# Gate stores on ACT's queue, loads in program order where the branch products begin, sums of h in program order, the first tile's norm weight by channel

## The chip, the cores and the metric

One core of one Trainium2 chip. The metric is the device time of one execution in microseconds (us). A core has TensorE (PE, matmuls), VectorE (DVE), ScalarE (ACT), GpSimd (POOL), SyncE (SP, which here only issues DMAs) and 16 DMA engines.

## What is computed

One layer of a decoder with three parallel mixers, 1024 tokens by 1024 channels, all in float32. Cut to what matters:

```python
h = RMSNorm_pre(x)                       # x * rsqrt(mean(x^2)) * g_pre
q,k,v,z_a, u,v_s,z_s, z_m,xBC,dt, gates = split(h @ W_in)
y_att = sliding_window_attention(q, k, v) * silu(z_a)
y_sg  = spatial_gate(u, v_s) * silu(z_s)
y_ssm = RMSNorm(ssd(conv(xBC), dt) * silu(z_m))
merged = sum_i sigmoid(gate_i) * (y_i @ W_br_i)
out = x + RMSNorm_post(merged @ W_out)
```

## The kernel before

Every float32 matrix is split into a high part (ACT casts it) and a low part (DVE subtracts, POOL for some of the weights), and a product is three matmuls per 128-channel step: high by high, high by low, low by high. TensorE executes its instructions in the order in which the program writes them. For the other engines the tile framework picks an order of its own, except inside `tc.manual_schedule(engines=...)`, where the engines named keep the program's order too.

The stages, in the order of TensorE:

1. Opening. Eight tiles of 128 tokens: `load_x` (L384), `norm` (sum of squares on ACT L392, `rs` on DVE and POOL, `hh` = x times `rs` times `gpre` on DVE L399), `flip` (eight transposes by TensorE L407, high part by ACT L410, low part by DVE L411). The first products (L141 to L143, weights `w_first`) begin as soon as tile 0 stands in `h`. The norm weight `gpre` is copied to all partitions by two DMAs that SP issues right behind the first tile of x.
2. Attention, with products of q, z_a, v_s and the gates filled in between; the last of the fillers are two `gate_unit`s (L116 to L118), whose results ACT takes out of PSUM into `vst` (L353).
3. Sums of h (L790 to L816). The products that follow use a scheme with seven products for eight (`PairStream`, L225 on), and need sums of blocks of h: for each of four steps `kt`, DVE makes four `r` (L797: high plus low part), POOL makes `x1` to `x4` from them (L800 to L803), and three of these are split into the blocks `S` (`split`, ACT L688 and DVE L689), the fourth later into the block `hB[1,0]`. `r` has one buffer each, `x1`, `x2`, `x4` two. Behind the four steps the first four weights of the stream are prepared (`whi` by ACT L253, `wlo` by DVE L228, differences of weights by POOL L223). The first pair product is L289 to L291.
4. The SSD chunks with pair products in between; DVE, ACT, POOL and SP keep the program's order here. Some of the pair products are gate logits: `tanh` on ACT (L693), and a store of 256 KB to `gate_dr` from SP's queue (L695), 44 of them. `evac` stores other results (L707).
5. The spatial gate (L1005 to L1060), whose results `yts` are stored to `y_dr` (L1043).
6. Branch products. `load_y` brings `y_dr` blocks back (SP L1080) and splits them (ACT L1091, DVE L1092), for y0 and y1 ahead of the loop and y2 to y7 behind the pools' change. The first unit of `br_unit` takes y0 and y1, then y2 and y3, and so on (L116 to L118). `load_w` (L93 to L100) brings its weights; `raw`, `whi` and `wlo` have three buffers each, which it shares with `PairStream`.
7. The product with `w_out`, the last norm and the store.

Of the kernel before, what the change touches and what calls it, by code (L numbers as in the profile page):

```python
# [11 lines left out]
F32 = mybir.dt.float32  # L12
# [28 lines left out]
def hybrid_kernel(ctx, tc, t, out):  # L41
# [24 lines left out]
    one = mhalf_row[:, 1:2]  # L66
    dsk, ng, bcv = mhalf_row[:, 2:18], mhalf_row[:, 18:34], mhalf_row[:, 34:58]
    bst = const.tile([P, NB, 4, 8], F32, name="bst")
    ssum = const.tile([P, 32], F32, name="ssum")
    acs, etot, dth, edec = (const.tile([P, NB, 32], F32, name=nm) for nm in ("acs", "etot", "dth", "edec"))  # L70

# [11 lines left out]
    def bcast_load(dst, src):  # L83
        nc.sync.dma_start(out=dst, in_=src.unsqueeze(0).broadcast_to([P, src.shape[-1]]))
# [287 lines left out]
    if True:  # L372

        with tc.tile_pool(name="xp", bufs=1) as xp:
# [5 lines left out]
            def load_x(tt):  # L380
                xt = xp.tile([P, D], F32, name="xt", bufs=2)
                for i in range(1 if tt else 2):
                    f = slice(i * 512, (i + 1) * 512) if tt == 0 else slice(0, D)
                    nc.sync.dma_start(out=xt[:, f], in_=t["x"][tt * P:(tt + 1) * P, f])  # L384
                return xt

            def norm(tt, xt):
                sq = xp.tile([P, D], mybir.dt.bfloat16, name="sq", bufs=1)
                ss = xp.tile([P, 2], F32, name="ss", bufs=2)
                for i in range(2):  # L390
                    f = slice(i * 512, (i + 1) * 512)
                    A.activation(sq[:, f], xt[:, f], AF.Square, accum_out=ss[:, i:i + 1])  # L392
                rs = xp.tile([P, 1], F32, name="rs", bufs=2)
                V.tensor_tensor(rs, ss[:, 0:1], ss[:, 1:2], op=ALU.add)
                rsqrt(rs, rs, 1.0 / D)
                hh = xp.tile([P, D], F32, name="hh", bufs=3)
                for i in range(2):
                    f = slice(i * 512, (i + 1) * 512)
                    V.scalar_tensor_tensor(hh[:, f], xt[:, f], rs, gpre[:, f], op0=ALU.mult, op1=ALU.mult)  # L399
                return hh  # L400

            def flip(tt, hh):
                for i in range(2):
                    ps = psum(ps_tr, "tr")
                    for j in range(4):
                        k = i * 4 + j
                        T.transpose(ps[:, j * P:(j + 1) * P], hh[:, k * P:(k + 1) * P], ident)  # L407
                    src = ps.rearrange("p (k s) -> p k s", k=4)
                    dst = [h[:, :, tt % 4 * P:(tt % 4 + 1) * P] for h in hB[tt // 4, i]]
                    A.copy(dst[0], src)  # L410
                    V.tensor_tensor(dst[1], src, dst[0].bitcast(F32), op=ALU.subtract)  # L411

            xts = {0: load_x(0)}
            for i in range(2):
                bcast_load(gpre[:, i * 512:(i + 1) * 512], t["g_pre"][i * 512:(i + 1) * 512])
            wfirst, hh = [], {}

            def first_w(i):
# [2 lines left out]
            with tc.manual_schedule(engines={mybir.EngineType.DVE, mybir.EngineType.Activation}):  # L421
                hh[0] = norm(0, xts.pop(0))
                first_w(0)
                first_w(1)
                xts[1] = load_x(1)
                flip(0, hh.pop(0))
                first_w(2)
                hh[1] = norm(1, xts.pop(1))
                first_w(3)
# [261 lines left out]
    def gate_pair(n):  # L691
        def tanh(b, d):
            A.activation(d, d, AF.Tanh, scale=0.5)  # L693
            i, half = NGATE + 2 * n + b % 10 - 1, b // 10 - 1
            nc.sync.dma_start(out=gate_dr[i, :, half * 512:(half + 1) * 512], in_=d)  # L695
            yield from ()

        def evac(b, d, after):
            pst.fresh.append(tanh(b, d[:, 4:]))
        return [t["w_gp"][n][k] for k in range(2)], evac  # L700
# [86 lines left out]
            pst.add(conv_pair(g, next(cv)) if kind == "x" else z_pair(g, next(z)) if kind == "z"  # L787
                    else zu_pair(next(zu)) if kind == "u" else gate_pair(next(gates)))

    with tc.tile_pool(name="bp", bufs=1, reuse_waits="tile") as bp:  # L790
        made = []
        for kt in range(5):
            if kt < 4:
                r = {}
                for ij, h in hB.items():
                    r[ij] = bp.tile([P, 512], F32, name="r%d%d" % ij)
                    V.tensor_tensor(r[ij], h[0][:, kt, :].bitcast(F32), h[1][:, kt, :].bitcast(F32), op=ALU.add)  # L797
                x1, x2, x4 = (bp.tile([P, 512], F32, name=f"x{i}", bufs=2) for i in (1, 2, 4))
                x3 = bp.tile([P, 512], F32, name="x3", bufs=4)
                G.tensor_tensor(x1, r[1, 0], r[1, 1], op=ALU.add)  # L800
                G.tensor_tensor(x2, x1, r[0, 0], op=ALU.subtract)
                G.tensor_tensor(x3, r[0, 0], r[1, 0], op=ALU.subtract)
                G.tensor_tensor(x4, r[0, 1], x2, op=ALU.subtract)  # L803
                made.append((x1, x2, x3, x4))
            st.fill(10.4)
            if kt > 0:
                x1, x2, _, x4 = made[kt - 1]
                for to, x in ((s1, x1), (s2, x2), (s4, x4)):
                    split(to, kt - 1, x)
        st.drain()  # L810

        for q in range(pst.AHEAD):
            pst._prepare(q)
        pst.prepared = pst.AHEAD
        for kt in range(4):
            split(hB[1, 0], kt, made[kt][2])  # L816
# [257 lines left out]
    def raw_tile(m):  # L1074
        return (py if m % 4 < 2 else pz).tile([P, S], F32, name=f"yraw{m % 4 // 2}", bufs=2)
# [42 lines left out]
        return ct_unit(t["w_br"][un * 8 + dd], rhs, evac, (2, 4, 5, 6, 7, KT) if k == dd == 0 else (KT,))  # L1118

    br = [br_unit(k, dd) for k in range(4) for dd in range(8)]  # L1120
    for n in range(NPY):
        ys[n] = load_y(n)
    st.add(*br[:8])
    st.loaded = st._load()
    pst.run(4)
    while pst.fresh or pst.waiting or pst.active:
        pst._work()
    es7.close()
    ph1.close()
    pz = ctx.enter_context(tc.tile_pool(name="pz", bufs=1, reuse_waits="tile"))  # L1130
    pools.append(pz)

    for n in (9, 10, 11):
        spare[n] = slot(n)
    pz.tile([P, 384], F32, name="pz_pad")
    for n in (5, 6, 7, 8):
        spare[n] = slot(n)
    merged.extend(pz.tile([P, S], F32, name=f"mg{i}") for i in range(4))
    for n in (2, 3):
        raws[n] = raw_tile(n)  # L1140
    for n in (2, 3, 4):
        spare[n] = slot(n)
    merged.extend(pz.tile([P, S], F32, name=f"mg{i}") for i in range(4, 8))
    for n in range(NPY, 8):
        ys[n] = load_y(n)
    for un in range(4):
        st.fill(5.2 * 8)
        if un < 3:
# [52 lines left out]
def _layout(inp):  # L1201
# [36 lines left out]
    for nm in ("q", "za"):  # L1238
# [2 lines left out]
    o["w_br"] = np.concatenate([ct(wb[:1024], 8), ct(wb[1024:], 8), ct(a["w_br_att"][0], 8),  # L1241
                                ct(a["w_br_sg"][0], 8)], 0)
    o["g_pre"] = a["norm_pre"][0]
    o["g_post"] = a["norm_post"][0]
    o["rel"] = a["rel_bias"][_buckets()].transpose(0, 2, 1)
    o["sinks"] = a["att_sinks"][0]
# [28 lines left out]
```

## Time and profile before

| | us |
|---|---|
| runs of the kernel before | 6930.69, 1812.04, 1818.29 |
| median of these | 1818.29 |
| profiled execution, its own time | 1813.3 |
| span of that execution | 1811.6 |
| TensorE busy in the span | 1744.7 |
| mean granted clock of TensorE | 0.99 |

The span is what the trace covers, from the first to the last instruction; the profiled execution's own time is 1.7 us longer. In the trace every instruction has a start, a length, its line and, in square brackets, how long its engine was idle before it and who ended that idle time. The rows that are used stand in a section below.

### The profile page before, as it was taken

To read this page: it belongs to the slowest core of one execution; us is meant where nothing else is said; L and a number is where in the kernel's file an instruction comes from. 1 tells how busy PE (TensorE), PEld (TensorE's weight loads), DVE (VectorE), ACT (ScalarE), POOL (GpSimd) and SP (SyncE) were. 2 spreads that over 40 slices of the span, in tenths; PEclk is the share of its full clock that TensorE was granted. 3 is DMA by queue.
4 is the path that set the end of the run, shared out by engine and by line. 5 is a ranking of instruction groups with operands and counts; after the bars stand their busy time and mean duration, and the time that the engine had idled before them with its cause. 6 is when DMAs were issued, how large, how long until landed. Compare 5 with 4: busy or idle time off the path is not lost. (4 is left out here: it accounts for less than half of the span.)

```text
span 1811.6 us, 26027 instructions
## 1 busy us (share of the span) xinstructions
PE 1744.7 (96%) x9181; PEld 1470.6 (81%) x9181; DVE 1271.1 (70%) x1781; ACT 842.0 (46%) x1883; POOL 843.7 (47%) x761
## 2 busy tenths in 40 slices
PE   7999999998999999999999999999889999999997
PEld 6888888897888877877887788887767888888897
DVE  6456676658998988899788978886775374444424
ACT  5245555534556666766577665542232212111221
POOL 1015566656665786777678765656324050000000
PEclk9999999999999999999999999999999999999999
DMA  6121111122334556445654564544786353533204
GB/s 228 63 79 48 47 59 40 52 82 67 105 105 145 164 176 197 144 129 171 196 160 141 162 194 153 166 137 125 245 277 242 108 189 125 171 116 93 82 24 163
DMA packets 165378, 243.28 MB, mean 134 GB/s; under 512 B 13153, under 2 KB 105601, under 8 KB 165121
## 3 DMA queue, kind: packets, MB, share of 16 engines
q1 hardware_dynamic: 165248, 241.63, 41.9%
q8 instruction: 73, 1.20, 0.3%
q14 instruction: 57, 0.46, 0.1%
HBM read 177.99 MB, written 63.59 MB: 133 GB/s over the span
## 5 line engine op out<-in xcount | busy, mean ns | idle before, releaser
L228 DVE TENSOR_TENSOR wlo<-raw,whi 128x512 fp32r<-128x512 f32 x195 | 193.6, 994 | 24.8 <-ACT whi L253 21.3
L116 PE MATMUL ps_mm<-y,whi 128*128 128x512 f32 x512 | 201.0, 393 | 7.7 <-ACT y L1091 7.7
L117 PE MATMUL ps_mm<-y,whi 128*128 128x512 f32 x512 | 201.1, 393 | 2.0 <-DVE y L1092 2.0
L118 PE MATMUL ps_mm<-y,wlo 128*128 128x512 f32 x512 | 200.6, 392 | 0.0
L289 PE MATMUL ps_mm<-h,whi 128*128 128x512 f32 x468 | 192.4, 411 | 3.7 <-ACT vst L353 3.7
L98 ACT CAST whi<-raw 128x1024 fp32r<-128x1024 f32 (+1 forms) x69 | 71.5, 1038 | 248.6 <-PE ps_mm L117 233.2
L291 PE MATMUL ps_mm<-h,wlo 128*128 128x512 f32 x468 | 183.0, 391 | 0.0
L290 PE MATMUL ps_mm<-h,whi 128*128 128x512 f32 x468 | 182.8, 391 | 0.0
L253 ACT CAST whi<-raw 128x512 fp32r<-128x512 f32 x195 | 118.8, 613 | 93.2 <-POOL raw L223 72.3
L89 POOL TENSOR_TENSOR rso<-rso,mhalf_row 128x1 f32<-128x1 f32 x8 | 4.4, 545 | 323.2 <-DVE rso L88 323.2
L289 PE MATMUL ps_mm<-S,whi 128*128 128x512 f32 x352 | 142.1, 404 | 4.6 <-DVE tp L301 3.5
L753 DVE SCALAR_TENSOR_TENSOR acc<-tp,wcv,acc 128x512 f32<-128x512 f32 x144 | 145.1, 1027 | 1.7
L291 PE MATMUL ps_mm<-S,wlo 128*128 128x512 f32 x352 | 137.5, 391 | 1.8 <-DVE wlo L228 1.8
L290 PE MATMUL ps_mm<-S,whi 128*128 128x512 f32 x352 | 137.3, 390 | 0.0
L223 POOL TENSOR_TENSOR ts<-raw 128x512 f32<-128x512 f32 x78 | 123.9, 1589 | 17.0 <-DVE wlo L228 12.4
L116 PE MATMUL ps_mm<-h,whi 128*128 128x512 f32 x304 | 120.9, 398 | 1.2 <-ACT vst L353 1.2
L116 PEld LDWEIGHTS ps_mm<-y,whi 128*128 128x128 f32 x512 | 96.9, 189 | 28.8 <-ACT y L1091 8.8
L1115 DVE SCALAR_TENSOR_TENSOR tm<-gld,ps_mm 128x512 f32<-128x512 f32 x48 | 32.9, 686 | 123.1 <-PE ps_mm L118 123.1
L117 PE MATMUL ps_mm<-h,whi 128*128 128x512 f32 x304 | 118.6, 390 | 0.0
L118 PE MATMUL ps_mm<-h,wlo 128*128 128x512 f32 x304 | 118.5, 390 | 0.0
L117 PEld LDWEIGHTS ps_mm<-y,whi 128*128 128x128 f32 x512 | 96.9, 189 | 23.6 <-DVE y L1092 3.6
L118 PEld LDWEIGHTS ps_mm<-y,wlo 128*128 128x128 f32 x512 | 97.1, 190 | 20.2
(242 smaller groups left out, 4873.5 us busy)
## 6 DMA issues: line engine op xcount, KB each, us to landing
seg<-acs_dr SPq DMA_DIRECT2D x64, 256.0 KB, 4.2
raw<-in_w_br_dram SPq DMA_DIRECT2D x32, 512.0 KB, 4.4
yraw<-y_dr SPq DMA_DIRECT2D x32, 512.0 KB, 4.7
gld<-gate_dr SPq DMA_DIRECT2D x32, 512.0 KB, 3.5
raw<-in_w_xbc_dram SPq DMA_DIRECT2D x24, 512.0 KB, 3.9
raw<-in_w_gp_dram SPq DMA_DIRECT2D x22, 512.0 KB, 4.4
gate_dr<-tp SPq DMA_DIRECT2D x44, 256.0 KB, 3.4
raw<-in_w_zm_dram SPq DMA_DIRECT2D x16, 512.0 KB, 4.5
```

Source lines behind the costliest of these rows:

```text
L98: A.copy(hi, raw)
L116: T.matmul(ps, lhsT=whi[:, ks], rhs=rhs(0, kt, half), start=kt == 0, stop=False)
L117: T.matmul(ps, lhsT=whi[:, ks], rhs=rhs(1, kt, half), start=False, stop=False)
L118: T.matmul(ps, lhsT=wlo[:, ks], rhs=rhs(0, kt, half), start=False, stop=kt == KT - 1)
L223: G.tensor_tensor(b[out], b[x], b[y], op=ALU.subtract)
L228: V.tensor_tensor(lo, src, hi.bitcast(F32), op=ALU.subtract)
L253: A.copy(hi, src)
L289: T.matmul(o, lhsT=hi[:, ks], rhs=h0, start=kt == 0, stop=False)
L290: T.matmul(o, lhsT=hi[:, ks], rhs=h1, start=False, stop=False)
L291: T.matmul(o, lhsT=lo[:, ks], rhs=h0, start=False, stop=kt == 3)
L753: V.scalar_tensor_tensor(acc, d[:, 1 + tap:513 + tap], wcv[:, ti, tap:tap + 1], acc, op0=ALU.mult, op1=ALU.add)
L1115: V.scalar_tensor_tensor(tm, gt[0][:, fs], 1.0, ps, op0=ALU.add, op1=ALU.mult)
```

## The change

Four edits:

- The 44 stores of gates (256 KB each) are issued from ACT's queue, behind the `tanh` that writes the data, and not from SP's.
- From the first `load_y` to the last before the branch loop, SP keeps the program's order.
- In the section with the sums of h, DVE, ACT and POOL keep the program's order.
- Tile 0 leaves the norm weight out of `hh`. `flip` applies it behind the transpose, where a channel is a partition: eight ACT instructions with a per-partition scale and eight DVE instructions, each 128x128, in place of two and two of 128x512. The weight comes as `gcol`, eight columns of 128 numbers placed into a free column of `bst`, by one DMA of 1024 separate 4-byte elements behind x0. `gpre` is loaded by one DMA behind tile 1 of x.

```diff
+    gcol = bst[:, :, 0, 6:7]
...
-                    V.scalar_tensor_tensor(hh[:, f], xt[:, f], rs, gpre[:, f], op0=ALU.mult, op1=ALU.mult)
+                    if tt == 0:
+                        V.tensor_scalar(hh[:, f], xt[:, f], rs, None, op0=ALU.mult)
+                    else:
+                        V.scalar_tensor_tensor(hh[:, f], xt[:, f], rs, gpre[:, f], op0=ALU.mult, op1=ALU.mult)
...
-                    A.copy(dst[0], src)
-                    V.tensor_tensor(dst[1], src, dst[0].bitcast(F32), op=ALU.subtract)
+                    if tt == 0:
+                        for j in range(4):
+                            g = gcol[:, i * 4 + j, :]
+                            A.activation(dst[0][:, j, :], src[:, j, :], AF.Copy, scale=g)
+                            V.scalar_tensor_tensor(dst[1][:, j, :], src[:, j, :], g, dst[0][:, j, :].bitcast(F32),
+                                                   op0=ALU.mult, op1=ALU.subtract)
+                    else:
+                        A.copy(dst[0], src)
+                        V.tensor_tensor(dst[1], src, dst[0].bitcast(F32), op=ALU.subtract)
...
             xts = {0: load_x(0)}
-            for i in range(2):
-                bcast_load(gpre[:, i * 512:(i + 1) * 512], t["g_pre"][i * 512:(i + 1) * 512])
+            nc.sync.dma_start(out=gcol, in_=t["g_col"])
...
                 xts[1] = load_x(1)
+                bcast_load(gpre, t["g_pre"])
...
-            nc.sync.dma_start(out=gate_dr[i, :, half * 512:(half + 1) * 512], in_=d)
+            nc.scalar.dma_start(out=gate_dr[i, :, half * 512:(half + 1) * 512], in_=d)
...
-    with tc.tile_pool(name="bp", bufs=1, reuse_waits="tile") as bp:
+    with tc.tile_pool(name="bp", bufs=1, reuse_waits="tile") as bp, tc.manual_schedule(
+            engines={mybir.EngineType.DVE, mybir.EngineType.Activation, mybir.EngineType.Pool}):
...
-    for n in range(NPY):
-        ys[n] = load_y(n)
-    st.add(*br[:8])
-    st.loaded = st._load()
-    pst.run(4)
+    with tc.manual_schedule(engines={mybir.EngineType.SP}):
+        for n in range(NPY):
+            ys[n] = load_y(n)
+        st.add(*br[:8])
+        st.loaded = st._load()
+        pst.run(4)
...
-    for n in range(NPY, 8):
-        ys[n] = load_y(n)
+        for n in range(NPY, 8):
+            ys[n] = load_y(n)
```

TensorE's order is the same in both kernels. The other engines' orders differ at three places.

ACT in the section with the sums of h, before. `S` from `x` is the high part of a sum, `vst` what comes out of the gate units, `whi` from `raw` or `ts` (L253) a weight of the stream:

```order
L253 CAST whi<-raw 128x512
L362 COPY vst<-ps_mm 128x256
L253 CAST whi<-raw 128x512
L688 CAST S_4292<-x_4561 128x512
L688 CAST S_4290<-x_4562 128x512
L688 CAST S_4294<-x_4563 128x512
L353 ACTIVATE vst<-ps_mm 128x256 x2
L688 CAST S_4292<-x_4645 128x512
L688 CAST S_4290<-x_4646 128x512
L688 CAST S_4294<-x_4647 128x512
L253 CAST whi<-ts 128x512
L353 ACTIVATE vst<-ps_mm 128x256 x2
```

The same place after, from the second gate unit's `vst` on (L354, L700 and L254 are L353, L688 and L253 of before):

```order
L354 ACTIVATE vst<-ps_mm 128x256 x4
L700 CAST S_4304<-x_4456 128x512
L700 CAST S_4302<-x_4457 128x512
L700 CAST S_4306<-x_4458 128x512
L700 CAST S_4304<-x_4575 128x512
L700 CAST S_4302<-x_4576 128x512
L700 CAST S_4306<-x_4577 128x512
L700 CAST S_4304<-x_4659 128x512
L700 CAST S_4302<-x_4660 128x512
L700 CAST S_4306<-x_4661 128x512
L254 CAST whi<-raw 128x512 x3
```

All four `vst` of the second gate unit now stand ahead of the `S` of the second, third and fourth step, and the stream's first weight stands behind the last of them; before, two weights were cast ahead of the third step's `S`.

DVE at the same section, after (before, the twelve `r` of the second to fourth step stand where their buffers allow, between the `S`):

```order
L701 TENSOR_TENSOR S_4305<-x_4456,S_4304 128x512
L701 TENSOR_TENSOR S_4303<-x_4457,S_4302 128x512
L701 TENSOR_TENSOR S_4307<-x_4458,S_4306 128x512
L810 TENSOR_TENSOR r_4651<-h_105,h_106 128x512
L810 TENSOR_TENSOR r_4653<-h_107,h_108 128x512
L810 TENSOR_TENSOR r_4655<-h_109,h_110 128x512
L810 TENSOR_TENSOR r_4657<-h_111,h_112 128x512
```

and before:

```order
L797 TENSOR_TENSOR r_4559<-h_111,h_112 128x512
L689 TENSOR_TENSOR S_4293<-x_4442,S_4292 128x512
L689 TENSOR_TENSOR S_4291<-x_4443,S_4290 128x512
L689 TENSOR_TENSOR S_4295<-x_4444,S_4294 128x512
L797 TENSOR_TENSOR r_4637<-h_105,h_106 128x512
L797 TENSOR_TENSOR r_4639<-h_107,h_108 128x512
```

Here the two kernels read alike: the fourth step's `r` stand behind the second step's `S`. What differs is when that `S` can run, which ACT's order says.

DVE where the branch products begin, before (`tp` is a result of the pair products, `y` from `yraw` a low part of y, `wlo` from `raw` (L99) a branch weight, `wlo` from `ts` (L228) the last weight of the stream):

```order
L301 TENSOR_TENSOR tp<-tp,ps_mm 128x512
L99 TENSOR_TENSOR wlo<-raw,whi 128x1024
L228 TENSOR_TENSOR wlo<-ts,whi 128x512
L301 TENSOR_TENSOR tp<-tp,ps_mm 128x512
L316 TENSOR_TENSOR tp<-tp,ps_mm 128x512
L318 TENSOR_TENSOR tp<-tp,ps_ax 128x512
L1092 TENSOR_TENSOR y_13349<-yraw_13346,y_13348 128x1024
L99 TENSOR_TENSOR wlo<-raw,whi 128x1024
L1092 TENSOR_TENSOR y_13355<-yraw_13352,y_13354 128x1024
```

and after:

```order
L302 TENSOR_TENSOR tp<-tp,ps_mm 128x512 x2
L317 TENSOR_TENSOR tp<-tp,ps_mm 128x512
L319 TENSOR_TENSOR tp<-tp,ps_ax 128x512
L1105 TENSOR_TENSOR y_13366<-yraw_13363,y_13365 128x1024
L1105 TENSOR_TENSOR y_13372<-yraw_13369,y_13371 128x1024
L100 TENSOR_TENSOR wlo<-raw,whi 128x1024
L229 TENSOR_TENSOR wlo<-ts,whi 128x512
L100 TENSOR_TENSOR wlo<-raw,whi 128x1024
L323 TENSOR_TENSOR tp<-tp,ps_mm 128x512
L100 TENSOR_TENSOR wlo<-raw,whi 128x1024
L1105 TENSOR_TENSOR y_13476<-yraw_13473,y_13475 128x1024
```

The stream's last low part moves behind four `tp`, y0, y1 and the first branch weight.

SP at the same place, before:

```order
L1080 DMA yraw_13346<-y_dr 128x1024
L1080 DMA yraw_13352<-y_dr 128x1024
L695 DMA gate_dr<-tp 128x512
L95 DMA raw<-in_w_br_dram 128x1024
L84 DMA rsb<-rs_dr 128x1024
L695 DMA gate_dr<-tp 128x512
L1080 DMA yraw_13474<-y_dr 128x1024
L695 DMA gate_dr<-tp 128x512
L1080 DMA yraw_13478<-y_dr 128x1024
L95 DMA raw<-in_w_br_dram 128x1024
L1080 DMA yraw_13456<-y_dr 128x1024
L1080 DMA yraw_13457<-y_dr 128x1024
```

and after:

```order
L1093 DMA yraw_13363<-y_dr 128x1024
L1093 DMA yraw_13369<-y_dr 128x1024
L96 DMA raw<-in_w_br_dram 128x1024 x3
L85 DMA rsb<-rs_dr 128x1024
L96 DMA raw<-in_w_br_dram 128x1024 x3
L1093 DMA yraw_13473<-y_dr 128x1024
L1093 DMA yraw_13474<-y_dr 128x1024
L1093 DMA yraw_13491<-y_dr 128x1024
L1093 DMA yraw_13495<-y_dr 128x1024
```

Two branch weights that were issued ahead of y0 and y1 now stand behind them, and all six stand ahead of y2 (yraw_13473 after, yraw_13456 before).

## Rows read from the trace of the kernel before

**Rows 1.** The page's first part: busy time, share of the span, instructions of each engine.

```profile
PE 1744.7 (96%) x9181; PEld 1470.6 (81%) x9181; DVE 1271.1 (70%) x1781; ACT 842.0 (46%) x1883; POOL 843.7 (47%) x761
```

**Rows 2.** Waits of PE: line, who was waited for, us in total, times, longest.

```profile
PE ps_tr L407 <- DVE hh L399: 10.5, 3, 7.9
PE ps_mm L116 <- ACT y L1091: 7.7, 1, 7.7
...
PE ps_mm L141 <- ACT h L410: 3.4, 2, 1.9
...
PE ps_mm L142 <- DVE h L411: 1.5, 1, 1.5
```

**Rows 3.** Stretches of time: us, busy us of each engine, PE's granted clock, DMA share, GB/s.

```profile
49.20:52.60 3.40, 3.03 (x9) 2.91 (x10) 2.00 (x5) 0.00 (x0) 0.00 (x0) 0.50 0.18 58
425.90:437.00 11.10, 7.26 (x29) 4.91 (x28) 8.00 (x11) 7.42 (x17) 3.39 (x3) 1.00 0.16 55
1349.70:1366.70 17.00, 8.83 (x21) 5.93 (x20) 6.92 (x6) 5.72 (x6) 0.00 (x0) 0.50 0.91 327
```

**Rows 4.** Timeline of PE, sums of h: start, us, instruction, idle before it and releaser.

```profile
420.44 0.50 PE L116 MATMUL ps_mm<-h,whi 128*128 128x512 f32 x1 [1.22 <-ACT vst L353]
...
429.54 0.50 PE L289 MATMUL ps_mm<-h,whi 128*128 128x512 f32 x1 [3.35 <-ACT vst L353]
```

**Rows 5.** Timeline of ACT, DVE and POOL in the sums of h.

```profile
427.79 0.62 ACT L688 CAST S<-x 128x512 fp32r<-128x512 f32 x1 [1.06 <-POOL x L803]
...
428.83 0.65 ACT L353 ACTIVATE vst<-ps_mm 128x256 f32<-128x256 f32 x2
...
400.05 0.69 DVE L797 TENSOR_TENSOR r<-h,h 128x512 f32<-128x512 f32 x1 [1.19 <-POOL x L801]
...
396.84 1.29 POOL L800 TENSOR_TENSOR x<-r,r 128x512 f32<-128x512 f32 x1
...
426.16 1.60 POOL L803 TENSOR_TENSOR x<-r,x 128x512 f32<-128x512 f32 x1
```

**Rows 6.** Timeline of DVE, ACT and PE where the branch products begin.

```profile
1341.77 0.68 DVE L228 TENSOR_TENSOR wlo<-ts,whi 128x512 fp32r<-128x512 f32 x1
...
1347.72 1.22 DVE L1092 TENSOR_TENSOR y<-yraw,y 128x1024 fp32r<-128x1024 f32 x1
...
1358.83 1.04 ACT L1091 CAST y<-yraw 128x1024 fp32r<-128x1024 f32 x1 [1.49 <-DMA yraw<-y_dr]
...
1343.65 0.39 PE L291 MATMUL ps_mm<-h,wlo 128*128 128x512 f32 x1
...
1359.93 0.79 PE L116 MATMUL ps_mm<-y,whi 128*128 128x512 f32 x1 [7.70 <-ACT y L1091]
```

**Rows 7.** The page's DMA issues: times, KB each, median us from issue to landing.

```profile
yraw<-y_dr SPq DMA_DIRECT2D x32, 512.0 KB, 4.7
```

**Rows 8.** Timeline of the opening, and a 128x128 instruction of DVE from stage 5.

```profile
7.08 0.75 DVE L399 SCALAR_TENSOR_TENSOR hh<-xt,rs,gpre 128x512 f32<-128x512 f32 x1 [1.74 <-DMA gpre<-in_g_pre_dram]
...
9.10 0.75 DVE L399 SCALAR_TENSOR_TENSOR hh<-xt,rs,gpre 128x512 f32<-128x512 f32 x1 [1.27 <-DMA gpre<-in_g_pre_dram]
...
10.05 1.88 ACT L98 CAST whi<-raw 128x832 fp32r<-128x832 f32 x2 [5.09 <-DMA raw<-in_w_first_dram]
...
11.84 1.07 ACT L410 CAST h<-ps_tr 128x512 fp32r<-128x512 f32 x2
...
12.47 0.29 PEld L141 LDWEIGHTS ps_mm<-whi,h 128*128 128x128 f32 x1 [1.85 <-ACT h L410]
...
19.09 1.94 PE L407 MATMUL ps_tr<-ident,hh 128*128 128x128 f32 x8 [1.71 <-DVE hh L399]
...
1336.17 0.35 DVE L1033 SCALAR_TENSOR_TENSOR sgb<-ps_tr,lnb,sgb 128x128 f32<-128x128 f32 x1
```

**Rows 9.** Stores of gates: SP's wait for ACT, and the page of line 695.

```profile
SPq L695 <- ACT tp L693: 40.3, 25, 4.4
...
L695 SPq DMA_DIRECT2D gate_dr<-tp x44: 319/322/506, 546.0 to 1350.2; - x44
```

More of the change, by code (lines that the diff above doesn't have):

```diff
@@ L1120, in hybrid_kernel @@
     br = [br_unit(k, dd) for k in range(4) for dd in range(8)]
-    for n in range(NPY):
-        ys[n] = load_y(n)
-    st.add(*br[:8])
-    st.loaded = st._load()
-    pst.run(4)
[L1126 to L1143, printed above, removed]
-    for n in range(NPY, 8):
-        ys[n] = load_y(n)
+    with tc.manual_schedule(engines={mybir.EngineType.SP}):
[4 more added lines that the diff above has]
+        pst.run(4)
+        while pst.fresh or pst.waiting or pst.active:
+            pst._work()
+        es7.close()
+        ph1.close()
+        pz = ctx.enter_context(tc.tile_pool(name="pz", bufs=1, reuse_waits="tile"))
+        pools.append(pz)
+        for n in (9, 10, 11):
+            spare[n] = slot(n)
+        pz.tile([P, 384], F32, name="pz_pad")
+        for n in (5, 6, 7, 8):
+            spare[n] = slot(n)
+        merged.extend(pz.tile([P, S], F32, name=f"mg{i}") for i in range(4))
+        for n in (2, 3):
+            raws[n] = raw_tile(n)
+        for n in (2, 3, 4):
+            spare[n] = slot(n)
+        merged.extend(pz.tile([P, S], F32, name=f"mg{i}") for i in range(4, 8))
+        for n in range(NPY, 8):
+            ys[n] = load_y(n)
     for un in range(4):
@@ L1243, in _layout @@
     o["g_pre"] = a["norm_pre"][0]
+    o["g_col"] = a["norm_pre"][0].reshape(KT, P, 1).transpose(1, 0, 2)
     o["g_post"] = a["norm_post"][0]
```

## The prediction

> **What bounds the kernel.** I read the page's busy times first, then PE's waits, then the timelines around the largest of these. TensorE is busy 96% of the span [rows 1], and its order is the same in both kernels, so the time is TensorE's work plus its idle time. Span less busy is 1811.6 - 1744.7 = 67 us, and 12.5 of these lie ahead of the first product [rows 8]. No single cause holds much of the rest: the longest waits are 10.5 us for `hh` in the opening, 7.7 for a block y, 3.4 and 1.5 for `h` [rows 2]; two waits of 1.22 and 3.35 us stand in the sums of h [rows 4]. So the change can give back at most the stalls at its own three places, and where it puts an instruction on the path it costs directly. A second price hangs on a stall: in two stretches the granted clock is 0.50, that is 1.2 GHz in place of 2.4 [rows 3]. One of them holds the 7.70 us wait; PE restarts at 1359.93 [rows 6] and full clock is back at 1366.7, 6.8 us at half pace, which costs 3.4. The 3.35 us wait in the sums stands in a stretch at 1.00 [rows 3], so a short one costs only itself.
>
> **Sums of h.** The edit adds and removes no instruction; it only fixes the order on ACT, DVE and POOL. Before, ACT made the sums' high parts and two weights of the stream while the gate units ran, and took the gate units' results out late: that is the pair of waits for `vst`, 1.22 and 3.35 [rows 4]. Both go: ACT now takes them out as they come. So PE ends the second gate unit at 425.0 (429.54 - 3.35 - 1.22). What is late next is the chain to the first pair product, as the order shows: all four `vst` of the second gate unit, then the second step's three `S`, then (DVE) the fourth step's `r`, which stand behind those `S`, then (POOL) the fourth step's four x, then the last `S` and only then the first weight. By the rows' durations [rows 5]: `vst` 0.65, three casts at 0.52 to 0.62, DVE's low part of the third 0.7: 428.0. Four `r` at 0.69: 430.7. Four x at 1.29 to 1.60: 435.9 to 437.1. One cast for `S`, one for the weight, 0.62 each: 437.1 to 438.3. I take 437.7, against 429.54 before: +8.2. PE then idles from 425.0 to 437.7, 12.7 us. That is longer than the 7.70 us behind which the clock was halved, so I add the 3.4 us: +11.6. Bounds: +13 if the weight differences on POOL, now behind the sums, hold up the third product by one more of its 1.60; and -4.6 if I misread the chain and only the two waits go. I take the +11.6, since every step has its row and no other work stands between the gate units and the stream on PE.
>
> **Where the branch products begin.** SP now issues y0, y1, six branch weights, then y2 to y7. Before, PE stopped 7.70 us for y2's high part, which ACT made at 1358.83 behind y4 and y5 [rows 6]; with y2 and y3 ahead of those the order is right. But two things come ahead of them. First, DVE: the low part of the stream's last weight ran at 1341.77, and PE used it at 1343.65 [rows 6]. Now it stands behind y0, y1 and the first branch weight, whose load SP issues only behind y1. Before, y1's low part ended at 1347.72 + 1.22 = 1348.9, with one weight's low part ahead of it; without that one, 1347.7. Then 1.22 for the weight (a low part of the size of y's), 0.68 for the stream's: about 1349.6 to 1350.8. PE stops at 1343.65 for some 6.5 us. Second, y2's load stands behind the sixth weight, which needs a buffer that the third weight gives back, and that one waits for the stream's last product, now ending about 1352.5 (half pace included 1354.5). A cast and a low part, 1.04 + 1.22, then 4.7 us from issue to landing [rows 7] and y2's cast 1.04 bring 1362.5 to 1363, against 1358.83 + 1.04 before. So PE's wait moves and is divided in two, and the later of the ends is +3 us behind before's 1359.93. The half clock is paid once in both. Bounds: -12, if the long wait and half the 8.83 us that PE worked at half clock [rows 3] go; +8, if the three weights ahead of y2 add 1.6 us each (512 KB at the stretch's 327 GB/s) [rows 3]. I take +3.
>
> **First tile.** Before, `hh` of tile 0 waited 1.74 and 1.27 us for `gpre`, and the cast of the first weights 5.09 us for its load, to 10.05; the first product began at 12.47 [rows 8]. Without the 512 KB of `gpre` ahead of it the weight lands earlier and `hh` doesn't wait: the first product gains between 0 and 3.0, I take 2. Against this, two ACT casts (1.07 together) become eight in turn with eight DVE instructions of 128x128, each about 0.35 [rows 8], with a hand-over between: 8 x 0.7 = 5.6 us. Behind them on ACT stand the third weight's cast and tile 1's squares, which release `hh` 1 and so the transposes at 19.09, where PE already waited 1.71 [rows 8]. They come 5.6 - 1.07 - 2 = 2.5 us later. In tiles later on, SP's order shifts; tile 7 may come in time, which would save 1.9 + 1.5 us of waits [rows 2] and the 1.7 us that 3.40 us of half clock cost [rows 3]. I take about two thirds of these 5.1, 3.5, so the part is 2.5 - 3.5 = -1; the 2 us of the earlier start are in the 2.5, since PE has to stop for tile 1 anyway. Bounds: -7 and +5. The new load `gcol` stands in no row: below, it costs nothing, above it takes 4.7 us as a 512 KB load does [rows 7], and it is issued early enough for either; I take nothing. The Trainium skill, "DMA: Bandwidth & Descriptors", section "Rules for kernel authors", says that a load with a strided last dimension becomes one descriptor per element; no run here shows its price.
>
> **Gate stores.** 44 issues of 0.32 us are 14 us of ACT's time, and ACT is idle 54% of the span [rows 1, 9]. The cover for it is that no wait for a plain ACT result stands long in the SSD stage; without the cover it costs up to 6 us. SP loses 40.3 us of waiting for `tanh` [rows 9], at most 4.4 at a time, and its loads come earlier; but no DMA stands among PE's long waits [rows 2], so this pays for nothing: 0, bounds -2 and +6. The Trainium skill, same page, section "Issuing engines are not separate DMA queues", speaks against a gain too: moving an issue saves the issuing sequencer's time only. By that it would be 0, by the row at most the 2 us.
>
> **Sum.** +11.6 + 3 - 1 + 0 = +13.6 on the profiled execution's 1813.3: 1827 us. That execution lies 5 us under the median of the runs shown, 1818.29, and between that run and the one of 1812.04.
>
> **Rivals.** *The order does what it is meant to (faster).* One mechanism: the instructions in program order find their inputs ready, and PE's stalls at the three places vanish. For it: each of them is an order by which something needed early stood late. Against it: the chain of the sums above. Price: 4.6 us of waits for `vst`; 7.7 and half of 8.83 at the branches, 12.1; 3.4 + 1.5 + 1.7 in the opening, 6.6. That is 23 us, 1790. It decides if the first pair product starts before 429.54. *No net change.* The branches gain what the sums lose: -12 + 11.6, 1813. For it: y2 and y3 do come first. Against: DVE's order there. *ACT becomes late (slower still).* A store on ACT's queue that has to wait for anything holds up every cast behind it; for 25 stores at 3.4 us, a store's own time to landing being of that order [4.7 for twice the size, rows 7], 85 us would stop ACT of which I count ACT's busy share, 46% [rows 1], as reaching PE through the weights and results behind it: 39 us on top of the 13.6, 1866. Against it: the data are made by ACT itself just ahead, so the store has its data when it is reached. It decides if ACT's idle time in the SSD stage is put down to DMAs.
>
> **How the numbers follow.** The forecast's case 0.58, no net change 0.18, the faster rival 0.16, the slower 0.08. The range holds 8 in 10: 1798 to 1843; it takes in no net change and the more likely half of the faster case, and the bounds of the sums and branches together. The likeliest case's own range is 1818 to 1836. A difference of 2%, 36 us, is about what a measurement of this kernel can tell from no change. Faster by that needs under 1782, more than all stalls named: 0.02. Slower needs over 1854, some two thirds of the slower rival: 0.05. Within: 0.93.
>
> **What would show it.** Right: PE idle for over 10 us ahead of the first pair product, released by the cast of a weight, and half clock behind it; a wait of L291 for `wlo` of some 6 us just ahead of the branch products; y2 still waited for. Wrong: the first pair product within 4 us of the second gate unit's end; y2 in place when PE asks; idle time of ACT on its own stores.

## The result and the profile after

| | us |
|---|---|
| changed kernel, median of 5 runs | 1824.72 (1824.0 to 1827.06) |
| kernel before, median of 5 runs beside it | 1812.04 |
| ratio | 1.0066, 95% interval 1.0053 to 1.0079 |
| span of the profiled execution | 1823.0 (before 1811.6) |

The change costs 0.66%, 12 us. That is within the 2% which the prediction took as what can be told from no change; with an interval from 0.53 to 0.79%, it is nevertheless clear of no change. The comparisons leave the execution of 6930.69 us out.

The page of the changed kernel, busy time of each engine, answers to [rows 1]:

```profile
PE 1747.3 (96%) x9181; PEld 1475.7 (81%) x9181; DVE 1258.8 (69%) x1787; ACT 846.4 (46%) x1889; POOL 838.4 (46%) x761
```

TensorE worked 2.6 us longer with the same 9181 instructions; the other 8.8 of the 11.4 us of span are idle time. PE's waits say which (line, who was waited for, us in total, times, longest), against [rows 2]:

```profile
PE ps_mm L290 <- ACT whi L254: 14.4, 1, 14.4
PE ps_tr L412 <- DVE hh L402: 6.8, 1, 6.8
PE ps_mm L292 <- DVE wlo L229: 6.7, 3, 4.9
...
PE ps_tr L412 <- DVE hh L404: 5.9, 1, 5.9
PE ps_mm L117 <- ACT y L1104: 5.1, 1, 5.1
...
PE ps_tr L892 <- DMA bcch<-bc_dr: 2.4, 3, 0.8
```

One wait of 14.4 us is new: the first pair product for the cast of its weight. The two waits for `vst` are gone, and so is the one of 7.7 us for y2; in its place stand 4.9 for `wlo` and 5.1 for y2.

The chain to that first product, from the timelines of ACT, DVE, POOL and PE (start, us, instruction, idle before it and its releaser), answers to [rows 4, 5]:

```profile
423.52 0.66 ACT L354 ACTIVATE vst<-ps_mm 128x256 f32<-128x256 f32 x2 [4.78 <-issue]
424.06 3.21 ACT L700 CAST S<-x 128x512 fp32r<-128x512 f32 x6
...
436.65 0.62 ACT L700 CAST S<-x 128x512 fp32r<-128x512 f32 x1 [2.72 <-POOL x L816]
437.18 1.13 ACT L254 CAST whi<-raw 128x512 fp32r<-128x512 f32 x2
...
424.71 1.90 DVE L701 TENSOR_TENSOR S<-x,S 128x512 fp32r<-128x512 f32 x3 [6.57 <-ACT S L700]
426.53 2.49 DVE L810 TENSOR_TENSOR r<-h,h 128x512 f32<-128x512 f32 x4
428.93 1.89 DVE L701 TENSOR_TENSOR S<-x,S 128x512 fp32r<-128x512 f32 x3
...
429.16 2.78 POOL L813 TENSOR_TENSOR x<-r,r 128x512 f32<-128x512 f32 x1 [5.72 <-DVE r L810]
432.02 1.26 POOL L814 TENSOR_TENSOR x<-x,r 128x512 f32<-128x512 f32 x1
433.25 1.71 POOL L815 TENSOR_TENSOR x<-r,r 128x512 f32<-128x512 f32 x1
434.92 1.71 POOL L816 TENSOR_TENSOR x<-r,x 128x512 f32<-128x512 f32 x1
...
437.84 0.79 PE L290 MATMUL ps_mm<-h,whi 128*128 128x512 f32 x1 [14.41 <-ACT whi L254]
```

Read it from below: PE starts when the weight is cast, the cast follows the last `S`, that one POOL's fourth x, the four x the four `r`, the `r` the low parts of the second step's `S`, and these the `vst` of the second gate unit. No two links lie beside each other. POOL had been idle for 5.72 us when the chain reached it.

Behind it the clock is halved, as the stretches show (us, busy us of PE, PEld, DVE, ACT, POOL, PE's granted clock, DMA share, GB/s), the second and third of them at the branch products:

```profile
437.80:441.00 3.20, 3.16 (x7) 2.06 (x8) 1.80 (x3) 0.74 (x2) 1.91 (x3) 0.50 0.00 0
...
1359.00:1363.50 4.50, 4.42 (x10) 3.46 (x11) 1.16 (x2) 0.18 (x1) 0.00 (x0) 0.50 0.83 257
1372.10:1376.00 3.90, 3.39 (x7) 2.23 (x8) 3.80 (x4) 3.14 (x3) 0.00 (x0) 0.50 0.78 292
```

Where the branch products begin, PE, DVE and SP of the changed kernel, answers to [rows 6]:

```profile
1353.77 0.39 PE L291 MATMUL ps_mm<-h,whi 128*128 128x512 f32 x1
1359.08 0.79 PE L292 MATMUL ps_mm<-h,wlo 128*128 128x512 f32 x1 [4.92 <-DVE wlo L229]
1372.15 0.80 PE L117 MATMUL ps_mm<-y,whi 128*128 128x512 f32 x1 [5.08 <-ACT y L1104]
...
1356.06 1.23 DVE L1105 TENSOR_TENSOR y<-yraw,y 128x1024 fp32r<-128x1024 f32 x1 [0.49 <-ACT y L1104]
1357.20 1.22 DVE L100 TENSOR_TENSOR wlo<-raw,whi 128x1024 fp32r<-128x1024 f32 x1
1358.34 0.69 DVE L229 TENSOR_TENSOR wlo<-ts,whi 128x512 fp32r<-128x512 f32 x1
...
1358.45 7.53 SPq L96 DMA_DIRECT2D raw<-in_w_br_dram  x3
1366.03 8.96 SPq L1093 DMA_DIRECT2D yraw<-y_dr  x6
```

DVE makes y1, the branch weight and then the low part PE waits for, without a gap; SP's three later weights take from 1358.45 to 1365.98, and y2 is issued behind them.

Where each loss falls is read best from the starts of the same instructions in both traces, since PE's order is the same:

| start of | before | after | shift | of this stage |
|---|---|---|---|---|
| first product | 12.47 | 10.40 | -2.07 | -2.07 |
| first gate unit in front of the sums | 402.72 | 401.48 | -1.24 | +0.83 |
| first pair product | 429.54 | 437.84 | +8.30 | +9.54 |
| the matmul of `xde` near 1124 | 1124.01 | 1134.99 | +10.98 | +2.68 |
| last product with y | 1708.65 | 1720.86 | +12.21 | +1.23 |
| end of the span | 1811.6 | 1823.0 | +11.4 | -0.8 |

Two of these are larger than what traces of kernels differ by anyway: the earlier first product (12.11 to 12.64 in the six traces with the old opening, 9.75 to 10.57 in the eight with the new one) and the +9.54. The sums take 26.81 or 26.82 us in all six traces that have their old order. But from the first pair product to the `xde` near 1124 the kernel before takes 694.47 us, the shortest of the six, and the other five take 694.82 to 697.14, among them 697.05 for the one whose only edit is SP's order, far behind that stage; the changed kernel's 697.15 is at the upper end. From there to the last product with y the seven kernels with the old order of these loads take 583.66 to 585.99, and the changed kernel 586.10.

### The profile page after: what moved, and what is told of

It is laid out like the page before. It is cut to its first block, busy times and chain, and to the rows that moved or that the text cites. A ratio compares the mean times of both kernels' runs of the same rounds, so it can differ in the third digit from the quotient of the medians.

```text
span 1823.0 us, 26005 instructions
## 1 busy us (share of the span) xinstructions
PE 1747.3 (96%) x9181; PEld 1475.7 (81%) x9181; DVE 1258.8 (69%) x1787; ACT 846.4 (46%) x1889; POOL 838.4 (46%) x761
## 5 line engine op out<-in xcount | busy, mean ns | idle before, releaser
L290 PE MATMUL ps_mm<-h,whi 128*128 128x512 f32 x468 | 193.6, 414 | 14.4 <-ACT whi L254 14.4
L99 ACT CAST whi<-raw 128x1024 fp32r<-128x1024 f32 (+1 forms) x69 | 71.5, 1038 | 246.7 <-PE ps_mm L118 231.1
L254 ACT CAST whi<-raw 128x512 fp32r<-128x512 f32 x195 | 118.7, 613 | 95.9 <-POOL raw L224 73.9
L290 PEld LDWEIGHTS ps_mm<-h,whi 128*128 128x128 f32 x468 | 89.2, 191 | 35.6 <-ACT whi L254 15.1
```

The costliest lines, as they stand in the source:

```text
L99: A.copy(hi, raw)
L254: A.copy(hi, src)
L290: T.matmul(o, lhsT=hi[:, ks], rhs=h0, start=kt == 0, stop=False)
```

## The experiments

Each run's ratio is to the kernel before on the same chip. First the four edits apart.

**Sums of h alone** (on the kernel before):

```diff
-    with tc.tile_pool(name="bp", bufs=1, reuse_waits="tile") as bp:
+    with tc.tile_pool(name="bp", bufs=1, reuse_waits="tile") as bp, tc.manual_schedule(
+            engines={mybir.EngineType.DVE, mybir.EngineType.Activation, mybir.EngineType.Pool}):
```

> The kernel before with one edit: DVE, ACT and POOL keep the program's order in the sums of h. My theory (this edit alone carries the loss): the first pair product about 8.3 us later than before, half clock behind it, +10 us in all, 1821 to 1823 against a kernel before of 1812. Rival (the loss is spread over the edits, and a late start of the stream is caught up in the SSD stage): under +6 us.

1825.38 us, ratio 1.0066 (1.0050 to 1.0082). The stage from gate unit to first pair product is 439.40 - 403.04 = 36.36 us long, to the hundredth what the whole change shows (437.84 - 401.48), against 26.82 before. This edit alone carries a loss as large as the whole. From the gate unit to the first `xde` of the SSD stage, so with the half clock behind the wait, it is 181.37 us here and 181.46 in the changed kernel, against 170.48 to 171.78 in the six traces with the old order of the sums: 9.6 to 11.0 us more.

```profile
PE ps_mm L289 <- ACT whi L253: 14.4, 1, 14.4
```

That is the same wait of 14.4 us in the list of PE's waits.

**The other three without it** (on the changed kernel):

```diff
-    with tc.tile_pool(name="bp", bufs=1, reuse_waits="tile") as bp, tc.manual_schedule(
-            engines={mybir.EngineType.DVE, mybir.EngineType.Activation, mybir.EngineType.Pool}):
+    with tc.tile_pool(name="bp", bufs=1, reuse_waits="tile") as bp:
```

> The changed kernel with the sums of h back in the framework's order; the other three edits stay. My theory: 1824.7 less 10, so 1814 to 1815, +2 on the kernel before (branches +2, opening -1, gate stores +1). Rival (loss is spread): 1818 or more.

1815.74, ratio 1.0009 (0.9998 to 1.0020). The stage is 26.81 us again. The rival, a loss that is spread, falls: without the order of the sums no loss can be told.

**Tile 0's norm weight alone** (the edits on `hh`, `flip`, `gcol` and `gpre` of the diff above, on the kernel before):

> The kernel before with one edit: tile 0's norm weight by channel. My theory: -1 us by the start of the stage behind the opening (347.39 for 348.38 in the changed kernel's trace), 1811. Rival (the eight and eight small instructions cost more than the start gives): +1 to +3. Either may lie within what five rounds can tell, so the trace's starts decide.

1812.74, ratio 0.9990 (0.9980 to 1.0001): not to be told from no change. The trace shows first product and first gate unit at 10.31 and 399.04, but a single trace does not settle this term: kernels that share the old opening begin the gate unit between 398.11 and 403.61. Over all traces of this study the mean is 401.8 for the six with the old opening and 400.4 for the eight with the new one. These 1.4 us are less than the spread of the six, so they are not shown to be the edit's.

**SP in program order alone** (the `manual_schedule` for SP of the diff above, on the kernel before):

> The kernel before with one edit: SP in program order from the first y to the last before the branch loop. My theory: a wait of 4 to 5 us for the stream's last low part, then one of about 5 us for y2, in all +2 to +3, 1814 to 1815. Rival (y2 and y3 ahead of y4 and y5 is a gain): 1806 or less.

1816.23, ratio 1.0010 (0.9999 to 1.0021), 1.8 us by the middle and not told from no change. The waits are those of the changed kernel, 5.5 for `wlo` and 4.5 for y2:

```profile
PE ps_mm L291 <- DVE wlo L228: 7.3, 3, 5.5
...
PE ps_mm L116 <- ACT y L1091: 4.5, 1, 4.5
```

**Gate stores alone** (the one line in `tanh`, on the kernel before):

> The kernel before with one edit: the 44 gate stores from ACT's queue. My theory (the issues lie in ACT's idle time): within 2 us of before, 1811 to 1815, PE's stalls in the SSD stage as before but for the short waits for bcch (3 of 0.8 us in the changed kernel). Rival (a store in ACT's queue holds up casts): +4 us or more, and PE waits for ACT in the SSD stage that before doesn't have.

1817.77, ratio 1.0014 (1.0003 to 1.0026), so 2.5 us slower, between 0.5 and 4.7, which does not decide between the two expectations. PE's waits for ACT in the SSD stage don't grow; those for the load `bcch` do in this trace, to 3.8 us from 0.7:

```profile
PE ps_tr L879 <- DMA bcch<-bc_dr: 3.8, 3, 3.0
```

That does not follow the edit, though: over all traces these waits are 0.6 to 3.8 us in the five kernels with the stores on ACT's queue and 0.7 to 1.7 in the nine without. From the first pair product to the `xde` near 1124 this trace takes 694.82 us against 694.47, so it does not show the 2.5 us; the traced execution, 1814.39, was itself 3.4 us under the median of its kernel. Where the 2.5 us fall stays open. The rival's sign, ACT idle until one of its own stores has landed, is there: 3.5 us ahead of `btok`, 2.3 ahead of a `tp` and 0.9 ahead of `rt`. The five kernels with the stores on ACT's queue have 4.7 to 12.3 us of such idle time, the nine others none. That it reaches PE is not shown.

The four alone add to 6.6 + 1.0 + 1.4 - 1.0 = 8.0 thousandths, 14.5 us, and the whole has 6.6; their intervals cover the difference.

Then the mechanism in the sums. **Program order kept, the filler halved** (on the changed kernel):

```diff
-            st.fill(10.4)
+            st.fill(5.2)
             if kt > 0:
```

> The changed kernel, program order in the sums of h kept, but the filler between two steps of the sums halved (5.2 in place of 10.4), so that the sums stand beside the gate units and not behind them. My theory (what costs is the place of the second step's casts behind the second gate unit): the first pair product follows the gate units within 1 us, near 425, no half clock; 12 to 14 us less than the changed kernel, 1811 to 1813. Rival (program order itself starves DVE, ACT or POOL there, wherever the filler stands): the first product still 5 us or more late, 1818 or more.

1813.02, ratio 0.9995 (0.9986 to 1.0004), less than the changed kernel by 11.7 us as the medians go and by 12.9 as the ratios go, and not told from the kernel before. `fill` writes down PE's filler work between two steps; with half as much each step's casts stand behind half a gate unit. The first product:

```profile
425.15 0.79 PE L290 MATMUL ps_mm<-h,whi 128*128 128x512 f32 x1 [3.47 <-ACT whi L254]
```

The 14.41 us are 3.47. So it was not program order that starved the engines, but the place in the program at which the order put the sums. Two points of the expectation missed: the wait is 3.47 and not within 1, and the clock did fall.

```profile
425.10:428.00 2.90, 2.85 (x6) 1.96 (x7) 1.70 (x3) 0.55 (x2) 1.67 (x2) 0.50 0.26 90
```

**The first two weights behind the second gate unit, ahead of the second step's casts** (on the changed kernel):

```diff
             st.fill(10.4)
+            if kt == 2:
+                pst._prepare(0)
+                pst._prepare(1)
+                pst._second()
             if kt > 0:
...
-        for q in range(pst.AHEAD):
+        for q in range(2, pst.AHEAD):
             pst._prepare(q)
```

> The changed kernel, but the first two weights of the stream are prepared right behind the second gate unit, ahead of the second step's casts; the sums' order stays. My theory (the weight's cast is the chain's last link, and the first two products need no sum): the first product near 425, then 5.5 us of two products, then a wait of 2 to 5 us for the block S2 of the fourth step; 7 to 10 us less than the changed kernel, 1815 to 1818. Rival (the blocks S bind, not the weight): no more than 3 us less, 1822 or more.

1821.21, ratio 1.0045 (1.0032 to 1.0059), 3.5 us less than the changed kernel (3.8 by the ratios), not 7 to 10; the rival was nearer. The first product starts at 424.81, as expected, but the wait moves to the third, which needs the blocks `S`:

```profile
441.32 0.79 PE L290 MATMUL ps_mm<-S,whi 128*128 128x512 f32 x1 [10.50 <-ACT whi L254]
```

The timelines of POOL and DVE say why it is 10.50 and not 2 to 5: the two weights' low parts on DVE and the differences on POOL pushed the fourth step back.

```profile
425.61 1.62 POOL L224 TENSOR_TENSOR raw<-raw,ts 128x512 f32<-128x512 f32 x1 [0.88 <-POOL ts L224]
427.19 1.74 POOL L224 TENSOR_TENSOR raw<-raw 128x512 f32<-128x512 f32 x1
432.92 2.49 POOL L813 TENSOR_TENSOR x<-r,r 128x512 f32<-128x512 f32 x1 [3.99 <-DVE r L810]
...
426.00 4.08 DVE L701 TENSOR_TENSOR S<-x,S 128x512 fp32r<-128x512 f32 x3
430.00 2.48 DVE L810 TENSOR_TENSOR r<-h,h 128x512 f32<-128x512 f32 x4
```

The same three low parts took 1.90 us in the changed kernel; here, while POOL ran, 4.08. The first x starts at 432.92 in place of 429.16.

Then the branches. **y2 and y3 in the buffers that y0 and y1 give back** (on the kernel before):

```diff
-        return (py if m % 4 < 2 else pz).tile([P, S], F32, name=f"yraw{m % 4 // 2}", bufs=2)
+        late = m % 8 > 3 if m < 8 else m % 4 > 1
+        return (pz if late else py).tile([P, S], F32, name=f"yraw{int(late)}", bufs=2)
...
-    for n in (2, 3):
+    for n in (4, 5):
         raws[n] = raw_tile(n)
```

> The kernel before with one edit: y2 and y3 take the two buffers that y0 and y1 give back, and y4 and y5 the later ones, so that y2 and y3 are loaded first without an order forced on SP. My theory (y2's place behind y4 and y5 is what PE waited for): y2's high part near 1355 and not 1359.9, 4 to 6 us less than before, 1806 to 1809. Rival (the DMA engines bind there, 91% busy, so the order of the loads doesn't matter): within 2 us of before.

1814.19, ratio 1.0010 (0.9999 to 1.0022). The expectation fell, and with it the thought that having y2 first is enough there. The long wait for y2 is gone; y2 is in place at 1352.7. But PE then stops for y2's low part, for y3 and so on, in eleven short waits around this place of at most 1.34 us:

```profile
1352.72 0.50 PE L116 MATMUL ps_mm<-y,whi 128*128 128x512 f32 x1 [1.05 <-ACT y L1092]
1353.98 0.50 PE L117 MATMUL ps_mm<-y,whi 128*128 128x512 f32 x1 [0.76 <-DVE y L1093]
1355.26 0.80 PE L116 MATMUL ps_mm<-y,whi 128*128 128x512 f32 x1 [0.55 <-ACT y L1092]
```

The stretches say what goes with it: the DMA share is 0.96 to 1.01 from 1348 to 1360.

```profile
1348.00:1352.00 4.00, 3.52 (x8) 2.48 (x8) 1.83 (x3) 1.01 (x2) 0.00 (x0) 0.59 0.96 368
1352.00:1356.00 4.00, 1.97 (x4) 0.77 (x4) 1.99 (x2) 1.71 (x2) 0.00 (x0) 0.83 0.98 318
1356.00:1360.00 4.00, 3.54 (x9) 2.81 (x9) 1.63 (x2) 2.07 (x2) 0.00 (x0) 0.50 1.01 407
```

The first unit needs all eight blocks, and whichever comes first, the last comes at about the same time: ACT begins y7 at 1366.79, 22.2 us behind the first product with y, before at 1367.39, 21.5 us behind it. Two causes stand side by side, and no run tells them apart. One is the full DMA engines up to 1360. The other is a buffer: y6's load is issued only at 1360.09, before at 1361.16, as soon as DVE has made the low part of the third of y2 to y5. Fewer bytes or one more buffer were not tried.

**Three edits together**: tile 0, the halved filler, the exchanged buffers, with gate stores and SP as before.

> Three edits on the kernel before: tile 0's norm weight by channel, the sums of h in program order with the filler halved, y2 and y3 in the buffers of y0 and y1; gate stores on SP, SP in the framework's order. My theory: -1 in the opening, -4.6 for the waits for vst, -5 at the branches: 1800 to 1803. Rival (gains at one place are lost at the next): 1808 or more.

1812.20, ratio 0.9991 (0.9982 to 1.0000), hardly told from the kernel before. The rival was right: the sums keep the wait of 3.5 us, and the buffers give nothing.

**Halved filler, and two weights ahead of the third or of the second step's casts** (both with tile 0's edit, with gate stores and SP as before):

```diff
-            st.fill(10.4)
+            st.fill(5.2)
+            if kt == 3:
+                pst._prepare(0)
+                pst._prepare(1)
+                pst._second()
             if kt > 0:
...
-        for q in range(pst.AHEAD):
+        for q in range(2, pst.AHEAD):
             pst._prepare(q)
```

Ahead of the third step's (`kt == 3`):

> Two edits of the change on the kernel before, tile 0's norm weight by channel and the sums of h in program order with the filler halved; and two weights of the stream prepared ahead of the third step's casts. Theory (in the run with the filler halved, 3.47 us remained because the first weight stood behind the fourth step's S): the first product follows the gate units at once, the second too, then up to 2 us for the third weight; 2 to 3 us less than that run's stage of 25.4 us from gate unit to first pair product plus what follows; 1808 to 1811. Rival (the wait moves to the third product whole, as in the run with the weights first): 1813.

1808.70, ratio 0.9964 (0.9952 to 0.9976), as expected. The first product follows the gate units without a wait; what is left is 0.41 and 1.46 us at the third:

```profile
428.67 0.50 PE L290 MATMUL ps_mm<-S,whi 128*128 128x512 f32 x1 [0.41 <-ACT whi L254]
430.86 0.50 PE L292 MATMUL ps_mm<-S,wlo 128*128 128x512 f32 x1 [1.46 <-DVE wlo L229]
```

Ahead of the second step's (`kt == 2`):

> As the run beside it, but the two weights, and with them POOL's three differences of weights, stand ahead of the second step's casts. Theory: POOL's 4.9 us of differences fall into its idle time before the fourth step's x, so the third weight is in time as well: no wait over 1 us at the start of the stream, 1807 to 1810. Rival: the differences delay the fourth step's x by up to 4.9 us and PE waits for S: 1812 or more.

1809.65, ratio 0.9968 (0.9956 to 0.9979). The expected "no wait over 1 us" missed: the third product waits 2.52. The two places can't be told apart by time.

**The sums' part of it alone** (the diff above with `kt == 3` and program order on DVE, ACT and POOL, on the kernel before):

> One part of the best version alone on the kernel before: the sums of h in program order with the filler halved and two weights of the stream ahead of the third step's casts; tile 0 as before. Theory (the gain of the best version is the sums', and tile 0 adds about 1 us): the stage from gate unit to first pair product near 21.8 us in place of 26.8, 4 to 5 us less than before, 1809 to 1811. Rival (tile 0's edit carries the gain, since the stream's later waits give the sums' gain back): 1813 or more.

1808.85, ratio 0.9962 (0.9949 to 0.9976). The stage takes 423.63 - 401.84 = 21.79 us in place of 26.82, as expected. So the same edit that cost 12 us gains 7 when its filler is cut finer and the first weights stand earlier, and it is this that beats both kernels; tile 0 adds nothing that can be told. Of the 7 us the stage shows 5.0; where the rest falls is not shown.

## Why the prediction was right

Forecast 1827 from 1813.3 plus 13.6; measured 1824.72, 12.7 over the median beside it and 12 by the ratio. The place and the mechanism, the chain of the sums, were right. That the sum came so near is in part luck, for several of its terms were off, in both directions. Step by step:

- *Sums, the chain.* Right in every link and in its end: the first pair product was put at 437.7 and came at 437.84. Two errors cancel in that: the gate units ended at 437.84 - 14.41 = 423.4 and not 425.0, 1.24 of these 1.6 us because they began earlier, and the four x, sized at 1.29 to 1.60 each, took 7.47 us (429.16 to 436.63). The first of them took 2.78, beside the low parts that DVE made from 428.93 on; alone it takes 1.29. So idle ahead of the product was 14.41 and not 12.7. The Trainium skill, "SBUF — State Buffer", section "Who interferes with whom", says that only the port pair shared by VectorE and GpSimd makes these engines wait, as an exclusive lock; the 2.78 here and DVE's 4.08 for 1.90 in the run with the weights first agree with it.
- *Sums, the half clock.* Right that it falls; the 3.4 us added for it and the reason given were wrong. The prediction tied the half clock to the wait of 7.70 us and took the 3.35 us wait in the sums as free of it. But its own stretch at 0.50 [rows 3] begins at 1349.70, and the wait only at 1359.93 - 7.70 = 1352.23: the clock fell while PE worked, behind waits of 0.42 and 1.13 us. And that the wait of 3.35 us stood at full clock was a matter of the execution. With the same order on PE and the same wait, the stretch behind it is at 1.00 in two of six traces (before and the stores alone), at 0.50 from the start in two (without the sums, and SP alone), and in the last two it falls 1.3 to 1.5 us later. The kernel before at the branches, then the run without the sums and the run with the stores alone behind the wait of 3.35 and 3.34 us:

```profile
1350.00:1352.00 2.00, 2.00 (x6) 1.22 (x4) 0.67 (x1) 0.20 (x1) 0.00 (x0) 0.50 1.00 399
...
428.10:433.10 5.00, 4.99 (x12) 3.89 (x13) 2.80 (x5) 2.64 (x7) 1.60 (x1) 0.50 0.30 104
...
428.40:433.40 5.00, 4.59 (x18) 3.26 (x19) 2.79 (x5) 2.61 (x6) 1.61 (x1) 1.00 0.29 101
```

  In the changed kernel half pace lasts from 437.84 to 443.1, which costs some 2.6 us. Net of what the old order loses there to half clock or to a short second wait for `vst`, it is less: from the first pair product to the first `xde` the changed kernel takes 145.10 us and the run with the sums alone 145.01, the six traces with the old order 143.67 to 144.97. So the term is 0 to 1.4 us and not 3.4, while the stage itself grew by 9.54 and not 8.2. The two errors have opposite signs: the sums cost 9.6 to 11.0 us up to there, near the forecast's 11.6.
- *Sums, bounds.* The lower bound of -4.6 was about what an order could give: with the finer filler and the weights earlier the stage fell by 5.0.
- *Branches.* The two waits came as told. The one for the low part was taken as some 6.5 us and is 4.9, that for y2 came behind it. The net was taken as +3; it is +1.9 at y2 (1372.15 - 1359.93 = 12.22, of which 10.35 had come before, 1353.77 for 1343.42), +1.2 at the last product, 1.8 by the time of the edit alone, with an interval from -0.2 to 3.8. The half clock was to be paid once as before; it is paid behind both waits, with about 11 us of PE's work at 0.50 (1359.1 to 1364.2 and 1372.2 to 1378.5) against 8.83 [rows 3].
- *First tile.* The eight pairs were sized 8 x 0.7 = 5.6 us and took 5.7, from 9.99 to 15.71; the timeline of ACT and DVE shows the hand-over in turn, against [rows 8]:

```profile
9.99 0.36 ACT L418 ACTIVATE h<-ps_tr,bst 128x128 fp32r<-128x128 f32 x1
10.38 0.35 DVE L419 SCALAR_TENSOR_TENSOR h<-ps_tr,bst,h 128x128 fp32r<-128x128 f32 x1
10.77 0.37 ACT L418 ACTIVATE h<-ps_tr,bst 128x128 fp32r<-128x128 f32 x1 [0.42 <-DVE h L419]
...
20.86 1.97 PE L412 MATMUL ps_tr<-ident,hh 128*128 128x128 f32 x8 [5.89 <-DVE hh L404]
```

  The start gained 2.07 (taken: 2), tile 1's transposes came 1.77 later (taken: 2.5), and PE's wait ahead of them grew from 1.71 to 5.89. Tile 7 came in better time, as was hoped: its two waits of 1.94 and 1.54 us are one of 1.11, and the clock stays at 1.00 there. The net of -1 is not contradicted and not shown: the edit alone is 1.8 us faster by the middle, with an interval from -3.6 to +0.2.
- *Gate stores.* Taken as 0 with bounds -2 and +6; alone 2.5 slower. The reason, that a store has its data when ACT reaches it, left out that ACT also waits for stores to land: 6.7 us in the run with the stores alone, 4.7 in the changed kernel, one of the prediction's signs of being wrong. It is far from the rival's 85 us; the cause of the 2.5 is not shown.
- *The rivals.* No net change needed a gain of 12 us at the branches to pay for the sums; SP's order alone shows no gain (1.8 slower by the middle). The slower one, ACT held up by its stores, needed 39 us; the run with the stores alone has 2.5, and 4.7 at the interval's end.
- *The rival that all stalls go (1790).* Its reason held in the sums, where the stalls were an order's and a finer one than this change has took them away. At the branches, where 12 us were counted, neither of the two orders that were tried brought anything.

## What to carry to other kernels

Program order is as good as the grain at which the program is written: a step placed behind a long filler becomes one chain over four engines. Cutting the filler in two took back the 12 us of loss, and with the first two weights earlier as well it became a gain of 7. To price a changed order, name the last instruction that it sets behind the waiting engine's work and add up the links from there, with the durations that each has when its neighbour runs too. Before loads are reordered, look at the DMA share of the stretch and at the buffer that the last of them waits for: in the one run that tried it here, with the share near one, the better order only broke one wait into many. And before a few us in one trace are put down to an edit, see by how much the same stage differs between traces that don't have it.

## What was not expected of the hardware

- The clock fell to 0.50 behind a wait of 3.47 us (425.10 to 428.00 above), while before the same place was at 1.00 behind 3.35 [rows 3]. The length of the wait does not decide it: behind 3.34 to 3.36 us, with the same work of PE ahead, it was 1.00 in two traces, 0.50 in two, and fell a little later in two.
- The opening differs between executions by more than the edit on it: the same code begins the gate unit at 398.11 in one kernel's trace and at 403.61 in another's. The stage of the sums behind it repeats to 0.01 us: 26.81 or 26.82 in all six kernels that share its order.
- The load of `gcol`, 4 KB in 1024 separate elements, took 5.4 us to land, near what the 512 KB of `gpre` took beside it, 7.2, and over the 4.7 that the prediction had as its upper end; it came early enough all the same. What the separate elements cost of it is not shown: other loads of 8 to 16 KB in the opening took 4.5 to 8.3 us.
